# Splitting each weight tile with a casting DMA and an accumulating DMA in a one-core decoder step

## The chip, the cores and the metric

The kernel runs on one core of one Trainium2 chip. The metric is the device time of one execution in microseconds (us), the median of the runs.

## What is computed

One inference step of a decoder trunk with one layer, for a prompt of 1024 tokens and 8 sample tokens (T = 1032 in all), model width 1024, in float32:

```python
h = rms_norm(x, g_mix)
z = h @ w_in                                   # 1024 -> 6400
a_lin, a_gate, q, k, v, g_a, g_b = jnp.split(z, SPLITS, axis=-1)
u = a_lin * jax.nn.sigmoid(a_gate)
c, new_conv = causal_dwconv(hist_conv, u, w_dw, b_dw)      # 31 taps
out_a = jax.nn.silu(layer_norm(c, ln_g, ln_b)) @ w_conv_out
...                                            # attention: three dilated window groups of four heads
mix = jax.nn.sigmoid(g_a) * out_a + jax.nn.sigmoid(g_b) * out_b
x = x + mix @ w_out
up, new_ffn = causal_dwconv(hist_ffn, rms_norm(x, g_ffn) @ w_up, w_fdw, b_fdw)
gate, val = jnp.split(up, 2, axis=-1)
x = x + (jax.nn.silu(gate) * val) @ w_down
```

The sample rows also read caches of keys, values and convolution states. The outputs hold those caches shifted by one position, so the old rows are copied from DRAM to DRAM.

## The kernel before

**Products.** Every product is made in three passes, so that it keeps the accuracy of float32: a weight tile and the activations are each split into a high part, rounded to the type fp32r, and a low part, the float32 value less the high part. `product` (L193 to L206) adds, for every block of 128 input channels k, the matmuls high·high, high·low (of the activations) and low·high into one PSUM bank. The tokens stand in NC3 = 3 groups of CW = 344, and one weight tile of 128 x 1024 float32 (512 KB) gives 8 x 3 x 3 = 72 matmuls.

**Weights.** There are 134 such tiles: 50 of `w_in`, then 2, 8, 8, 44 and 22 of the other matrices. The first five (ag0, al0, ag1, al1, ag2) are loaded and split by code of their own. The other 129 go through `load_w`: `fetch_w` lets the SP queue load the tile to `raw` (two buffers), `split_w` makes `hi` on ScalarE with a Copy into fp32r and `lo` on VectorE as raw - hi. There are WB = 3 buffers each for `hi` and `lo`, so tile n can be written once the matmuls of tile n - 3 are done. Both instructions have a raised priority (EARLY).

**Caches.** `cache_jobs` is a list of copies from DRAM to DRAM (`o_k...`, `o_v...`, `o_convs`, `o_ffns`). Each third `load_w` (PACE = 3) takes one of them and puts it on the SP queue; `after(d, ...)` (L155) orders it behind the tile's own load d on that queue.

**The order of work.** The Tile framework schedules the program with a simulated timeline and fixes one order per engine. Each engine and each issuing queue (SP, and POOL, the GpSimd queue) works through its order strictly: an instruction that waits holds up everything behind it. A DMA also waits for the eighth one before it on its kind of queue. Four PSUM banks (tag "mm") hold the outputs of the input projection; VectorE empties those of the linear half `al` (L477, into `u`), ScalarE those of the gate `ag` (L474, into `sg`).

**What runs beside.** While the input projection runs on TensorE, VectorE does the 31-tap convolution (`conv_wide`, L484 to L503): 30 instructions for each of 8 channel blocks. Its first step, `history()` (L431), loads the convolution state with two DMAs on the SP queue (`hist`, L434), multiplies it by the taps (L437) and sums it (L441). The stores of `u`, the loads `cu` of the convolution and most of the other traffic between SBUF and DRAM are issued on POOL (L480, L488 and others).

The stages on TensorE follow each other as: first blocks ag0, al0, ag1, then al1, ag2 (to 68 us), then al2, ag3, al3, ... al7, the queries, keys and values q0, k0, v0, ... v5 with the attention between them, the gates ga and gb, the branch outputs, the output projection xo, and the ConvFFN with its blocks ug, uv and wd.

Of the kernel before, what the change touches and what calls it, by code (L numbers as in the profile page):

```python
# [10 lines left out]
F32 = mybir.dt.float32  # L11
# [5 lines left out]
P = 128  # L17
# [39 lines left out]
class Queue:  # L57
    """an engine; while `held` its instructions keep the order of the program"""

# [17 lines left out]
def trunk_step(ctx: ExitStack, tc: tile.TileContext, A: dict):  # L77
# [34 lines left out]
    def advance(queue):  # L112
        """one step of a stream of background work; an entry is a function (one step) or a generator"""
        while queue:
            if callable(queue[0]):
                queue.popleft()()
                return
            try:
                next(queue[0])
                return  # L120
            except StopIteration:
                queue.popleft()
# [25 lines left out]

    # ------------------------------------------------------------ weights and products
    cache_jobs = []  # L150
# [4 lines left out]
    def after(first, then):  # L155
        """orders two instructions of one queue"""
        if first is not None:
            tc.add_manual_dep(
                then.ins, first.ins.name,
                mybir.DependencyInfo(mybir.DependencyClass.NoSync, mybir.DependencyReason.DATA),  # L160
                reason="order",
            )
# [7 lines left out]
    def fetch_w(src, name):  # L170
        raw = wp.tile([P, 1024], F32, tag="raw", name=f"raw_{name}")
        return raw, nc.sync.dma_start(raw, src)
# [11 lines left out]
    def load_w(src, name, extra=False):  # L184
        raw, d = fetch_w(src, name)
        w = split_w(raw, name, extra)
        n_weights[0] += 1
        if n_weights[0] % PACE == 0 and cache_jobs:
            dst, s = cache_jobs.pop(0)
            after(d, nc.sync.dma_start(dst, s))  # L190
        return w

    def product(ps, w, off, xh, xl, c, ks=None, late=False):  # L193
        """three passes for every k; late: those with the weights' low part at the end"""
        n = len(xh)
        sl = cs(c) if isinstance(c, int) else c
        m = sl.stop - sl.start
        ks = ks or range(n)
        passes = [(k, i) for k in ks for i in range(3)]
        if late:  # L200
            passes = [(k, i) for k in ks for i in range(2)] + [(k, 2) for k in ks]
        for k, i in passes:
            wk = w[i // 2][:, (off + k) * P:(off + k + 1) * P]
            xk = (xl if i == 1 else xh)[k][:, sl]
            ins = nc.tensor.matmul(ps[:, :m], wk, xk, start=(k == 0 and i == 0), stop=(k == n - 1 and i == 2))  # L205
        return ins  # L206

    def mm_blocks(jobs, xh, xl):
        """jobs: (weights, first 128 rows in them, name, evacuation(c, psum)); group by group over all jobs."""
        for c in range(NC3):  # L210
            for w, off, name, evac in jobs:
                ps = bank(f"{name}_{c}")
                product(ps, w, off, xh, xl, c)
                evac(c, ps[:, :CW])
                pump()

    def mm_wide(jobs, xh, xl, order):
        """as mm_blocks, with one evacuation of all groups: evac(psum [128, 3, CW])."""
        tiles = [wide(name) for _, _, name, _ in jobs]
        for j, c in order:  # L220
            w, off, _, evac = jobs[j]
            product(tiles[j][:, c, :], w, off, xh, xl, c)
            if c == NC3 - 1:
                evac(tiles[j][:, :, :CW])
# [6 lines left out]

    # ------------------------------------------------------------ norms
    mean_col = const.tile([P, 1], F32, name="mean_col")
# [10 lines left out]
    def offsets(n):  # L244
        """the token tiles of n tokens; the last may overlap the one before"""
        return [*range(0, n - P + 1, P)] + [n - P] * (n % P > 0)
# [10 lines left out]
    def rsqrt(ps, tmp):  # L257
        """1 / sqrt(ps + EPS), with one Newton step after the approximate root"""
        y, r, u = tmp
        act.activation(y, ps, AF.Sqrt, bias=eps_col)  # L260
        dve.reciprocal(r, y)
        dve.scalar_tensor_tensor(u, r, -0.5, r, ALU.mult, ALU.mult)
        dve.scalar_tensor_tensor(y, ps, EPS, u, ALU.add, ALU.mult)
        dve.scalar_tensor_tensor(r, y, 1.5, r, ALU.add, ALU.mult)
        return r
# [5 lines left out]
    def spread(r, name, behind=None, n=CW, d=None):  # L271
        """[token, tile] -> the tokens' row over all partitions, in PSUM."""
        offs = offsets(n)
        m = len(offs)
        d = (scratch(f"diag_{name}", "sm", m * P) if d is None else d).rearrange("p (a b) -> p a b", a=m)
        dve.tensor_tensor(
            out=d,
            in0=ident.unsqueeze(1).broadcast_to([P, m, P]),
            in1=r.unsqueeze(2).broadcast_to([P, m, P]),
            op=ALU.mult,  # L280
        )
        ps = bank(f"sp_{name}", "s")
        for j, off in enumerate(offs):
            after(behind, nc.tensor.matmul(ps[:, off:off + P], onesm, d[:, j, :], start=True, stop=True))
        return ps[:, :n]
# [21 lines left out]

    # ------------------------------------------------------------ first norm
    x_in = A["xT"]
# [24 lines left out]

    # of the first weights the part that the first products need comes first
    raw0 = scratch("raw_ag0", "ca", T)[:, :1024]
# [13 lines left out]
    def scaled_split(c, ks=range(KB), g=G_MIX):  # L350
        """x · g in two parts; a token's factor is left to the evacuations"""
        for k in ks:
            xk = xs[k][:, cs(c)]
            act.activation(hh[k][:, cs(c)], xk, AF.Copy, scale=pv[:, g, k:k + 1])
            dve.scalar_tensor_tensor(hl[k][:, cs(c)], xk, pv[:, g, k:k + 1], hh[k][:, cs(c)].bitcast(F32),
                                     ALU.mult, ALU.subtract)
# [23 lines left out]

    # the first blocks' products do not wait for the norm's factors
    R1, R2 = (0, 1, 2), (3, 4)
# [39 lines left out]

    # ------------------------------------------------------------ constants and the caches' copies
    wdw = load_const("w_dw", [P, KB, 31])
# [34 lines left out]

    # ------------------------------------------------------------ branch A: GLU and wide convolution  # L460
    u_dram = [dram.tile([P, T], F32, name=f"u_dram{k}") for k in range(KB)]
# [6 lines left out]
    def glu(j, sg=None, u=None):  # L468
        """the gate's and the linear half's evacuation, and the stores"""
        sg = sg or slot(f"sg{j}")  # L470
# [50 lines left out]

    # ------------------------------------------------------------ branch B: attention
    def perm(ap, g):
# [37 lines left out]
    def attention_unit(g, p):  # L561
# [93 lines left out]
        def sample_scores():  # L655
            """the sample rows against the cached keys and their own"""
            kc = slot(f"kc{b}", F32, NS * (P + 1)).rearrange("p (b j) -> p b j", b=NS)
# [29 lines left out]
    def combine(p):  # L687
# [21 lines left out]
        nc.scalar.activation(st[:, 1:4], st[:, 1:4], AF.Exp)  # L709
        # samples: one softmax over the three groups' keys, which weighs the groups by their denominators  # L710
        sst = small.tile([2 * NS, 4], F32, tag="sst", name=f"sst{p}")
# [33 lines left out]
    def sample_out(p):  # L745
        """the sample rows' weighted values, with the weights spread over a head's channels"""
        while taps:
# [17 lines left out]

    # ------------------------------------------------------------ LayerNorm of the convolution's output
    c_norm = []
# [41 lines left out]

    # ------------------------------------------------------------ gates  # L810
    sa_dram = [dram.tile([P, T], F32, name=f"sa_dram{k}") for k in range(KB)]
# [127 lines left out]

    # the second norm's factor of a token is left to the evacuations  # L940
    h2h, h2l = mh, ml
# [14 lines left out]

    # ------------------------------------------------------------ ConvFFN
    def narrow_conv(o, z, name):
# [30 lines left out]
    def up_first(blocks):  # L989
        """the first blocks, group by group"""  # L990
        ws = [w_first] + [load_w(A["w_up"][o], name) for o, name in blocks[1:]]
# [39 lines left out]

    # ------------------------------------------------------------ last products and norm, group by group
    s3 = slot("s3")
# [54 lines left out]

    # the last group leaves with its tokens over the partitions, where their factor is a column
    turned, yg = [], {}  # L1090
# [161 lines left out]
```

## Time and profile before

| what | value |
|---|---|
| time, median of 2 runs | 1676.63 us (1675.12 and 1678.14) |
| span of the profiled execution, first to last instruction | 1673.9 us |
| the profiled execution's own time | not given apart from its span; the runs' median is 2.7 us above the span |
| TensorE matmul busy | 1654.8 us, 99% of the span |
| VectorE busy | 1081.3 us, 65% |
| ScalarE busy | 522.4 us, 31% |
| GpSimd busy | 113.8 us, 7% |
| moved by DMA | 197.40 MB, of which 141.99 MB on SP's queue and 53.81 MB on POOL's |

A busy share is an average over stages that have different limits. A copy from DRAM to DRAM counts once in the bytes moved. Matmul rows overlap: each shows 0.32 us, but one starts every 0.157 us.

### The profile page before, as it was taken

Reading aid. Unit: us, or ns where it says so; the run is one execution under the profiler, and the core shown is the slowest. Engines: PE = TensorE matmul, PEld = TensorE weight load, DVE = VectorE, ACT = ScalarE, POOL = GpSimd, SP = SyncE. Lnnn points to the kernel's source line nnn. Section 1 sums busy time; section 2 is a strip of 40 time slices with the busy share of each in tenths; the row PEclk is TensorE's granted clock in tenths of the full one; section 3 lists DMA queues with packets and bytes.
Section 4 is the critical chain, followed back from the end, with each engine's and each line's share of the span. In section 5 each row is a group of like instructions: output and inputs, shape, how many; then the busy total and the mean of one; then the engine's idle time right before and its main releaser. Section 6 shows DMA issues by size and latency. Waiting matters only on the chain.

```text
span 1673.9 us, 25134 instructions
## 1 busy us (share of the span) xinstructions
PE 1654.8 (99%) x10564; PEld 1615.6 (97%) x10564; DVE 1081.3 (65%) x1594; ACT 522.4 (31%) x889; POOL 113.8 (7%) x174
## 2 busy tenths in 40 slices
PE   8999999999999999999999999999999999999997
PEld 8999998898898999999999999999999999999997
DVE  5889998798996996754346554544543553553466
ACT  6411123344433324542224322212221221221243
POOL 0101011011111102110000000000000000000002
PEclk9999999999999999999999999999999999999998
DMA  8544322332335439783531221222221221222112
GB/s 296 187 127 128 119 88 80 100 104 65 103 132 174 155 134 294 222 319 124 216 114 45 80 74 68 76 82 82 76 76 64 101 76 66 74 101 75 65 54 102
DMA packets 69264, 197.40 MB, mean 118 GB/s; under 512 B 8080, under 2 KB 29616, under 8 KB 69152
## 3 DMA queue, kind: packets, MB, share of 16 engines
q1 hardware_dynamic: 53376, 141.99, 25.8%
q0 software_dynamic: 15776, 53.81, 9.6%
q8 instruction: 83, 1.36, 0.3%
q14 instruction: 29, 0.24, 0.0%
HBM read 164.29 MB, written 76.61 MB: 144 GB/s over the span
## 4 chain that ended last, share of the span: by engine, by line
PE 93%; DVE 2%; issue 2%; DMA 1%; ACT 0%; SPq 0%; POOL 0%; DVEq 0%; POOLq 0%; ACTq 0%
PE uv L205 14%; PE ug L205 14%; PE dn L205 12%; PE ga L205 6%; PE xo L205 5%; PE v L205 4%; PE k L205 4%; PE q L205 4%; PE al L205 4%; PE oa L205 4%; PE gb L205 4%; PE ag L205 3%; PE first L205 3%; PE s L603 2%; PE up L205 2%; PE dl L205 2%
## 5 line engine op out<-in xcount | busy, mean ns | idle before, releaser
L493 DVE SCALAR_TENSOR_TENSOR ca<-cu,c_w_dw,ca 128x1019 f32<-128x1019 f32 (+22 forms) x240 | 300.4, 1268 | 1.7
L205 PE MATMUL uv<-mh,hi_uv 128*128 128x344 f32 x504 | 161.2, 320 | 0.0
L205 PE MATMUL uv<-mh,lo_uv 128*128 128x344 f32 x504 | 160.9, 319 | 0.0
L205 PE MATMUL uv<-ml,hi_uv 128*128 128x344 f32 x504 | 160.5, 318 | 0.0
L205 PE MATMUL ug<-mh,hi_ug 128*128 128x344 f32 x480 | 153.4, 320 | 0.0
L205 PE MATMUL ug<-mh,lo_ug 128*128 128x344 f32 x480 | 153.2, 319 | 0.0
L205 PE MATMUL ug<-ml,hi_ug 128*128 128x344 f32 x480 | 152.8, 318 | 0.0
L205 PE MATMUL dn<-gh,lo_wd 128*128 128x344 f32 x456 | 145.8, 320 | 0.0
L205 PE MATMUL dn<-gl,hi_wd 128*128 128x344 f32 x456 | 145.6, 319 | 0.1
L205 PE MATMUL dn<-gh,hi_wd 128*128 128x344 f32 x456 | 145.6, 320 | 0.0
L923 DVE TENSOR_TENSOR xr<-dn,xr 128x1032 f32<-128x1032 f32 x42 | 51.8, 1233 | 99.0 <-PE dn L205 99.0
L205 PEld LDWEIGHTS uv<-ml,hi_uv 128*128 128x128 f32 x504 | 94.7, 188 | 0.0
L205 PEld LDWEIGHTS uv<-mh,lo_uv 128*128 128x128 f32 x504 | 94.7, 188 | 0.0
L205 PEld LDWEIGHTS uv<-mh,hi_uv 128*128 128x128 f32 x504 | 94.5, 188 | 0.0
L205 PEld LDWEIGHTS ug<-ml,hi_ug 128*128 128x128 f32 x480 | 90.2, 188 | 0.0
L205 PEld LDWEIGHTS ug<-mh,lo_ug 128*128 128x128 f32 x480 | 90.2, 188 | 0.0
L205 PEld LDWEIGHTS ug<-mh,hi_ug 128*128 128x128 f32 x480 | 90.0, 188 | 0.0
L205 PEld LDWEIGHTS dn<-gl,hi_wd 128*128 128x128 f32 x456 | 85.7, 188 | 0.4 <-DVE gl L67 0.4
L205 PEld LDWEIGHTS dn<-gh,lo_wd 128*128 128x128 f32 x456 | 85.6, 188 | 0.0
L205 PEld LDWEIGHTS dn<-gh,hi_wd 128*128 128x128 f32 x456 | 85.6, 188 | 0.0
L67 ACT ACTIVATE hi_ug<-raw_ug 128x1024 fp32r<-128x1024 f32 x22 | 23.4, 1064 | 144.3 <-PE dn L205 92.3
L67 ACT ACTIVATE hi_uv<-raw_uv 128x1024 fp32r<-128x1024 f32 x22 | 23.4, 1063 | 127.1 <-PE ug L205 83.9
(725 smaller groups left out, 4403.7 us busy)
## 6 DMA issues: line engine op xcount, KB each, us to landing
o_k<-cache_k SPq DMA_DIRECT2D x16, 1023.5 KB, 7.2
o_v<-cache_v SPq DMA_DIRECT2D x16, 1023.5 KB, 6.2
raw_ug<-w_up SPq DMA_DIRECT2D x22, 512.0 KB, 3.5
raw_uv<-w_up SPq DMA_DIRECT2D x22, 512.0 KB, 3.5
raw_wd<-w_down SPq DMA_DIRECT2D x22, 512.0 KB, 3.4
xrow<-x_rows SPq DMA_DIRECT2D x9, 512.0 KB, 6.0
x<-xT SPq DMA_DIRECT2D x24, 172.0 KB, 5.2
u_dram<-u POOLq DMA_DIRECT2D x8, 516.0 KB, 3.0
```

The lines of the kernel that those rows point to most:

```text
L67: ins = op(*args, **kwargs)
L205: ins = nc.tensor.matmul(ps[:, :m], wk, xk, start=(k == 0 and i == 0), stop=(k == n - 1 and i == 2))
L493: after(anchor[0], nc.vector.scalar_tensor_tensor(acc[:, d:SEQ], u[:, :SEQ - d], w[:, 30 - d:31 - d], acc[:, d:SEQ], ALU.mult, ALU.add))
L603: nc.tensor.matmul(sps[:, :nk], q[hs, i * P:(i + 1) * P], k[hs, k0:k0 + nk], start=True, stop=True)
L923: nc.vector.tensor_tensor(out=v3(t), in0=ps, in1=v3(t), op=ALU.add)
```

## The change

`load_w` no longer loads `raw`. A DMA on POOL loads the tile into `hi`, whose type is fp32r, so that this DMA casts. ScalarE then writes the negative of `hi` to `lo`, and a second DMA on POOL loads the same tile again and adds it to `lo`. VectorE has no part in it. The copy of the caches stays on SP, but is no longer ordered behind a weight load. The other lines of the diff take out comments; they and the longer `load_w` move the line numbers behind it by seven.

```diff
     def load_w(src, name, extra=False):
-        raw, d = fetch_w(src, name)
-        w = split_w(raw, name, extra)
+        if extra:
+            hi, lo = (ph[0].tile([P, T], F32R, tag="gl", name=f"{n}_{name}", bufs=GB)[:, :1024] for n in ("hi", "lo"))
+        else:
+            hi, lo = (wp.tile([P, 1024], F32R, tag=n, name=f"{n}_{name}", bufs=WB) for n in ("hi", "lo"))
+        d = nc.gpsimd.dma_start(hi, src)
+        with tc.high_priority(EARLY):
+            act.activation(lo, hi.bitcast(F32), AF.Copy, scale=-1.0)
+            nc.gpsimd.dma_start(lo, src, accum_op=ALU.add)
         n_weights[0] += 1
         if n_weights[0] % PACE == 0 and cache_jobs:
             dst, s = cache_jobs.pop(0)
-            after(d, nc.sync.dma_start(dst, s))
-        return w
+            nc.sync.dma_start(dst, s)
+        return hi, lo
```

Since the scheduler sets the orders, they move more than the diff tells. On the SP queue, behind the load of the last tile that `fetch_w` still loads (raw_ag2), there stood before:

```order
L172 DMA raw_ag2_293<-w_in 128x1024
L1127 DMA o_ffns<-state_ffn 128x8x44
L172 DMA raw_al2_823<-w_in 128x1024
L172 DMA raw_ag3_928<-w_in 128x1024
L172 DMA raw_al3_1023<-w_in 128x1024
L190 DMA o_k128<-cache_k128 128x8x254
L172 DMA raw_ag4_1120<-w_in 128x1024
L172 DMA raw_al4_1212<-w_in 128x1024
L434 DMA hist0_855<-conv_hist 128x960
L434 DMA hist1_888<-conv_hist 128x960
```

The same place of the SP queue now, where x4 and x16 are four and sixteen copies in a row:

```order
L172 DMA raw_ag2_293<-w_in 128x1024
L197 DMA o_k128<-cache_k128 128x8x254
L197 DMA o_v128<-cache_v128 128x8x254
L197 DMA o_k512<-cache_k512 128x2x1022 x4
L197 DMA o_v512<-cache_v512 128x2x1022 x4
L197 DMA o_k2048<-cache_k2048 128x2047 x16
L197 DMA o_v2048<-cache_v2048 128x2047 x16
L197 DMA o_convs<-state_conv 128x8x232
L1134 DMA o_ffns<-state_ffn 128x8x44
L441 DMA hist0_854<-conv_hist 128x960
L441 DMA hist1_887<-conv_hist 128x960
```

All 44 copies of the caches have moved together, ahead of the two loads of `hist`; before, two of them stood there.

On VectorE, where the outputs of al2 are multiplied into u2, the new order is:

```order
L484 TENSOR_TENSOR u2_818<-al2_0_828,sg2_153 128x344
L444 TENSOR_TENSOR hist0_854<-hist0_854,c_w_dw_790 128x240 x4
L484 TENSOR_TENSOR u2_818<-al2_1_858,sg2_153 128x344
L444 TENSOR_TENSOR hist1_887<-hist1_887,c_w_dw_790 128x240 x2
L448 TENSOR_REDUCE hsum_800<-hist0_854 128x32
L444 TENSOR_TENSOR hist1_887<-hist1_887,c_w_dw_790 128x240 x2
L504 SCALAR_TENSOR_TENSOR hr0_1335<-cu0_959,c_w_dw_790,hsum_800 128x8
L504 SCALAR_TENSOR_TENSOR hr1_1715<-cu1_1340,c_w_dw_790,hsum_800 128x8
L484 TENSOR_TENSOR u2_818<-al2_2_889,sg2_153 128x344
```

The multiplications of `hist0` stand between the evacuations of al2's first and second token group; before, they stood behind the second one's.

On POOL the new order at the same time is:

```order
L190 DMA hi_al2_823<-w_in 128x1024
L487 DMA u_dram0_801<-u0_150 128x1032
L488 DMA o_u<-u0_150 128x38
L190 DMA hi_ag3_927<-w_in 128x1024
L487 DMA u_dram1_802<-u1_152 128x1032
L488 DMA o_u<-u1_152 128x38
L190 DMA hi_al3_1021<-w_in 128x1024
L193 DMA lo_al2_824<-w_in 128x1024
L495 DMA cu0_959<-u_dram0_801 128x1032
L193 DMA lo_ag3_928<-w_in 128x1024
L495 DMA cu1_1340<-u_dram1_802 128x1032
L193 DMA lo_al3_1022<-w_in 128x1024
```

The three loads of `hi` and the three of `lo` are new on this queue; the accumulating load of al2's low part stands behind the store of u1, which waits for the products of ag2 and al1.

## Rows read from the trace of the kernel before

**Rows 1.** The page: the span, and busy time, share and instructions of each engine.

```profile
span 1673.9 us, 25134 instructions
...
PE 1654.8 (99%) x10564; PEld 1615.6 (97%) x10564; DVE 1081.3 (65%) x1594; ACT 522.4 (31%) x889; POOL 113.8 (7%) x174
```

**Rows 2.** TensorE's waits, longest first: us in total, times, longest.

```profile
PE first L205 <- ACT hh L67: 5.6, 1, 5.6
PE turned L1099 <- ACT yg L1095: 3.3, 2, 3.1
```

**Rows 3.** Timeline of TensorE: start, duration of one row.

```profile
68.06 0.32 PE L205 MATMUL al<-hh,hi_al 128*128 128x344 f32 x1
...
86.92 0.32 PE L205 MATMUL ag<-hh,lo_ag 128*128 128x344 f32 x1
```

**Rows 4.** Timeline of the SP queue: issue time, length of the issue.

```profile
43.46 0.33 SPq L172 DMA_DIRECT2D raw_ag<-w_in  x1
...
47.57 0.58 SPq L190 DMA_DIRECT2D o_k<-cache_k  x1
...
71.68 0.90 SPq L434 DMA_DIRECT2D hist<-conv_hist  x2
```

**Rows 5.** DMA issues: count, KB each, median us from issue to landing.

```profile
o_k<-cache_k SPq DMA_DIRECT2D x16, 1023.5 KB, 7.2
...
raw_ug<-w_up SPq DMA_DIRECT2D x22, 512.0 KB, 3.5
...
u_dram<-u POOLq DMA_DIRECT2D x8, 516.0 KB, 3.0
cu<-u_dram POOLq DMA_DIRECT2D x8, 516.0 KB, 5.1
...
cn<-c_dram POOLq DMA_DIRECT2D x8, 516.0 KB, 13.8
...
o_k<-cache_k SPq DMA_DIRECT2D x4, 1022.0 KB, 8.9
...
o_k<-cache_k SPq DMA_DIRECT2D x1, 1016.0 KB, 7.6
...
o_convs<-state_conv SPq DMA_DIRECT2D x1, 928.0 KB, 6.3
...
o_ffns<-state_ffn SPq DMA_DIRECT2D x1, 176.0 KB, 5.1
```

**Rows 6.** Windows: length, busy of five engines, PEclk, DMA share, GB/s (last two columns).

```profile
1027.00:1030.00 3.00, 3.00 (x21) 3.00 (x20) 1.83 (x3) 1.07 (x1) 0.00 (x0) 1.00 0.99 411
...
20.00:30.00 10.00, 10.00 (x67) 10.00 (x67) 7.93 (x20) 8.20 (x18) 0.00 (x0) 1.00 1.02 372
...
640.00:660.00 20.00, 20.00 (x130) 20.00 (x129) 13.73 (x30) 8.59 (x12) 5.81 (x11) 1.00 0.98 314
```

**Rows 7.** Timeline of VectorE around the convolution state.

```profile
75.82 0.52 DVE L477 TENSOR_TENSOR u<-al,sg 128x344 f32<-128x344 f32 x1 [0.24 <-PE al L205]
76.49 1.37 DVE L437 TENSOR_TENSOR hist<-hist,c_w_dw 128x240 f32<-128x240 f32 x4 [0.16 <-DMA hist<-conv_hist]
```

**Rows 8.** Timeline of POOL's issues after the first blocks.

```profile
68.18 0.58 POOL L480 DMA_DIRECT2D u_dram<-u  x1 [6.75 <-DVE u L420]
```

**Rows 9.** The two splitting instructions, by tile: duration ns min/median/max.

```profile
L67 ACT ACTIVATE hi_ug<-raw_ug x22: 1057/1063/1068, 865.2 to 1565.8; 128x1024 fp32r<-128x1024 f32 x22
L67 DVE TENSOR_TENSOR lo_ug<-raw_ug,hi_ug x22: 1215/1217/1226, 866.3 to 1567.1; 128x1024 fp32r<-128x1024 f32 x22
```

**Rows 10.** Timeline of ScalarE: the split of the last weight tile, wd53.

```profile
1622.70 1.06 ACT L67 ACTIVATE hi_wd<-raw_wd 128x1024 fp32r<-128x1024 f32 x1 [3.98 <-PE dn L205]
```

**Rows 11.** Windows of the attention stage: columns as in rows 6.

```profile
200.00:300.00 100.00, 100.00 (x629) 91.66 (x628) 90.35 (x127) 32.02 (x77) 11.54 (x16) 1.00 0.32 93
300.00:400.00 100.00, 100.00 (x654) 89.08 (x654) 85.02 (x160) 40.70 (x120) 13.26 (x17) 1.00 0.30 86
400.00:500.00 100.00, 100.00 (x664) 90.74 (x663) 90.44 (x165) 39.95 (x125) 13.01 (x21) 1.00 0.33 109
```

## The prediction

> **What bounds the kernel now.** I read the page's busy times first. TensorE is busy for 1654.8 of 1673.9 us [rows 1]. So at most 19 us could be won without taking matmuls away, and the change takes none. Next I read TensorE's waits: the longest are 5.6 us at the start and 3.3 us at the end [rows 2]. No weight is late anywhere in between. VectorE's 1081 us and ScalarE's 522 us are covered by TensorE, so what the change takes from them is worth nothing directly. The question is what it makes late. The timeline of TensorE gives the pace: from the first matmul of al2 at 68.06 us to the one at 86.92 us there are 120 matmuls, one per 0.157 us [rows 3]. A token group of 24 takes 3.8 us, a weight tile of 72 takes 11.3 us. With three buffers, tile n's buffer comes free two tiles before tile n is wanted: 22.6 us.
>
> **Part 1: work taken away.** 129 VectorE subtractions of 1.217 us go, 157 us in all; ScalarE keeps 129 copies of 1.063 us, now from `hi` to `lo` [rows 9]. Both lie beside TensorE. I put the gain at 0. The bound: between 200 and 500 us, where VectorE is about 90% busy, the weight-load row of TensorE idles 8.3 + 10.9 + 9.3 = 28.5 us [rows 11]. If all of that were VectorE's doing, 28.5 us come back.
>
> **Part 2: the two DMAs of a tile in steady state.** From a free buffer to a ready `lo` there are four steps: the casting load, ScalarE's copy, POOL's two issues of some 0.53 us each, and the accumulating load. The trace shows neither kind of load. The nearest row is POOL's 516 KB load `cu`, 5.1 us to landing; SP's 512 KB load takes 3.5, POOL's store 3.0, and its slowest load in traffic, `cn`, 13.8 [rows 5]. With `cu` for both: 5.1 + 1.1 + 1.1 + 5.1 = 12.4 us, against 22.6. With 13.8 for the accumulating one it is 21.1, still inside. I take 0 for the steady state. The cover is gone once that load takes over 22.6 - 7.3 = 15.3 us.
>
> Three places have less than 22.6 us. At the end of xo, three tiles are worked group by group. wo5's buffer comes free 7.6 us before xo ends, and uv0 is wanted 3.8 us after it: 11.4 us, so uv0 is about 1 us late. ug1's `hi` is queued on POOL behind uv0's `lo`, so it is issued 7.3 us after wo5 is free and ready at 7.3 + 12.4 = 19.7, wanted at 15.1: together 5 us. wd53 is the second: its buffer is freed just before ScalarE's 1622.70 us [rows 10], and four blocks of 440 tokens (12 matmuls each, 12 x 0.157 x 440/344 = 2.4 us) come before it, 9.6 us against 12.4: 3 us. Third, ScalarE waits for each casting load with its evacuations queued behind it, and in the attention stage TensorE follows ScalarE closely. Eighteen tiles q, k and v by 5.1 us would be 92 us if nothing hid it; four PSUM banks of 3.8 us each hide most, and I take 7. Together 15 us; the ends are 0 and 100.
>
> **Part 3: the copies of the caches lose their pace.** This is the large term. Before, each copy stood on SP's queue behind a weight load that waited for its buffer; the first one was issued at 47.57 us, and `hist` was issued at 71.68 us and used at 76.49 us [rows 4, 7]. Now SP has no weight loads left behind raw_ag2, and the 44 copies go out back to back, held only by the rule that eight are in flight. `hist0` stands behind all of them. On VectorE its multiplication stands ahead of al2's second evacuation, so VectorE waits, with everything behind it, until `hist0` has landed. al2 keeps two of the four PSUM banks, TensorE can still do ag3's first two groups, and then it stands at ag3's third.
>
> When does `hist0` land? The copies are 32 of 1023.5 KB, 8 of 1022, 2 of 1016, one of 928 and one of 176 (o_k's rows stand for o_v too) [rows 5]: 44,064 KB, or 45.1 MB. On SP, raw_ag2 and `hist0` add 1.0 MB. POOL's loads and stores of that time (u0, u1, cu0, cu1 and seven weight loads) add 11 x 0.52 = 5.8 MB. Sum 51.9 MB. The first copy is issued right behind raw_ag2's 43.46 us [rows 4]; with 1.1 us to the first byte, 44.9 us. (A 512 KB load lands after 3.5 us, of which 1.3 us is data at 411 GB/s; I put half the rest ahead and half behind.) The rate: a single copy moved at 411 GB/s with the DMA engines 99% busy, the start's mix of loads at 372, the busiest mixed 20 us at 314 [rows 6]. All three have full engines, so no faster rate is in sight. For some 130 us of unbroken traffic I take the middle one, 372: 139.5 us, landing at 185.5 us. The four multiplications (1.37 us) and the evacuation (0.52) [rows 7] let TensorE go on at 187.4 us. Before, it had done the same 120 matmuls at 86.9 us. Loss: 100.5 us. At 411 GB/s the loss is 87 us, at 314 it is 126.
>
> This wait hides another. lo_al2 stands on POOL behind the store of u1, issued before at 68.18 us [rows 8]. With four issues and a load among the copies it lands near 80 us, so al2 is 12 us late. But al2 and ag3's first two groups are then done by about 100 us, long before 185, so this costs nothing more.
>
> The Trainium skill (DMA: Bandwidth & Descriptors, section Latency and other measured facts) gives 207 to 214 GB/s per direction for DMA copies between HBM tensors. This case's single copy at 411 disagrees; no run here shows many in a row. By it the time would be that of rival A below.
>
> **The sum.** Span 1673.9 + 100.5 + 15 = 1789.4 us; the median lies 2.7 us above the span, so 1792 us. Its own range is 1676.6 + 87 - 28.5 + 8 = 1743 (fastest copies, all of part 1's bound, only the 8 us of the two tile places) to 1676.6 + 126 + 100 = 1903.
>
> **The rivals.**
> A, *many copies in a row run at half a single one's rate*. For it: the mixed window at 314 GB/s is already a quarter lower. Against: the single copy's rate came with the engines 99% busy, so the engines set it. At 206 GB/s the 45.1 MB take 219 us and POOL's share passes beside; `hist0` lands at 268 us, the loss is 183 us, the time 1676.6 + 183 + 15 = 1875.
> B, *the accumulating load takes over 15.3 us*. For it: nothing in the trace shows one. The Trainium skill (DMA: Bandwidth & Descriptors, Rules for kernel authors) says that an accumulating DMA reads its destination and writes it later; no run here shows that. Against: it would have to be three times `cu`. At four times, 20.4 us, a tile needs 27.7 us from free to ready, three buffers turn every (27.7 + 11.3) / 3 = 13.0 us, and 129 tiles lose 1.7 us each: 1792 + 219 = 2011.
> C, *VectorE was what paced TensorE, and its relief pays for the stall: not slower*. For it: VectorE is 90% busy from 200 to 500 us, and 157 us of it go. Against: TensorE's list has no long wait on VectorE, and the idle of its loads there is 28.5 us. It decides once more than 100.5 + 15 - 33.5 = 82 us come back, which gives 1710; with all 157 us back it is 1635.
> That the DMAs do not round as ScalarE did would change values, but neither the count nor the shapes of the matmuls, so not the time.
>
> **Chances.** The forecast 0.66, A 0.10, B 0.15, C 0.05, the rest 0.04 spread like the forecast. A change of 2%, 33.5 us, is about what a measurement of this kernel can tell from none. Forecast, A and B are all slower by more: with the rest 0.94 (a little less for unseen cover). C splits into 0.03 within 2% and 0.03 faster, rounded up. The range 1743 to 1903 holds the forecast and A and leaves out B and C, 0.2 together.
>
> **What would show it.** Right: the copies all issued between 44 and about 170 us at a full DMA share; VectorE's longest wait the one for `hist`, some 90 us; one gap on TensorE of that size in ag3, ending at 175 to 215 us, and afterwards the old pace of 11.3 us per tile. Wrong: TensorE waiting on `lo` tiles throughout (B); `hist` landing before 100 us with no gap; or TensorE in the attention stage visibly faster than before (C).

## The result, and the profile after

The changed kernel takes 1819.49 us (median of 2 runs, 1818.20 and 1820.79) against 1676.63: a ratio of 1.085 [1.082, 1.089], 143 us slower. The forecast was 1792 us, the range 1743 to 1903. The profiled execution's span is 1819.0 us, 145.1 more than the span of before.

The page's busy line, against [rows 1]:

```profile
span 1819.0 us, 25175 instructions
...
PE 1658.9 (91%) x10564; PEld 1622.2 (89%) x10564; DVE 944.6 (52%) x1465; ACT 524.7 (29%) x889; POOL 292.6 (16%) x432
```

TensorE has the same 10564 matmuls and only 4 us more of busy time, so nearly all of the 145 us is time in which it stands. VectorE lost 129 instructions (1594 to 1465), the subtractions, and 137 us; POOL rose from 114 to 293 us. TensorE's waits of after, which answer to [rows 2], and the longest of VectorE and POOL (in all, times, longest):

```profile
PE ag L212 <- DVE u L484: 105.7, 1, 105.7
PE al L212 <- DMA lo_al<-w_in: 12.6, 1, 12.6
PE ag L212 <- DMA hi_ag<-w_in: 6.3, 1, 6.3
...
PE gb L212 <- ACT sb L826: 5.6, 3, 4.2
PE gb L212 <- DMA lo_gb<-w_in: 4.6, 1, 4.6
```

```profile
DVE hist L444 <- DMA hist<-conv_hist: 117.5, 1, 117.5
```

```profile
POOL u_dram L487 <- DVE u L484: 119.7, 6, 115.5
```

One wait of 105.7 us on TensorE stands out. It names VectorE's `u`, and VectorE in turn waited 117.5 us for a DMA, the load of `hist`. POOL, with its next weight loads, stood 115.5 us behind the same `u`. The timelines of SP and VectorE say why. They answer to [rows 4, 7], where `hist` was issued at 71.68 us and used at 76.49:

```profile
32.68 0.74 SPq L197 DMA_DIRECT2D o_k<-cache_k  x1
...
59.59 72.01 SPq L197 DMA_DIRECT2D o_k<-cache_k  x16
134.56 50.85 SPq L197 DMA_DIRECT2D o_v<-cache_v  x16
188.61 0.60 SPq L197 DMA_DIRECT2D o_convs<-state_conv  x1
191.76 14.94 SPq L1134 DMA_DIRECT2D o_ffns<-state_ffn  x1
206.81 3.65 SPq L441 DMA_DIRECT2D hist<-conv_hist  x2
```

```profile
97.41 0.52 DVE L484 TENSOR_TENSOR u<-al,sg 128x344 f32<-128x344 f32 x1 [19.07 <-PE al L212]
...
215.39 1.37 DVE L444 TENSOR_TENSOR hist<-hist,c_w_dw 128x240 f32<-128x240 f32 x4 [117.47 <-DMA hist<-conv_hist]
216.68 0.51 DVE L484 TENSOR_TENSOR u<-al,sg 128x344 f32<-128x344 f32 x1
```

VectorE empties al2's first token group at 97.41 us. The next instruction in its order multiplies `hist0`, which lands at 215 us because all copies of the caches stand ahead of it on SP, the first issued at 32.68 us, the last by 206.7. al2's second group is emptied at 216.68, and TensorE goes on. The windows of that stretch (columns as in [rows 6]) show a core on which only the copies work:

```profile
120.00:140.00 20.00, 0.00 (x0) 0.00 (x0) 0.00 (x0) 0.00 (x0) 0.00 (x0) 0.50 1.02 321
...
180.00:200.00 20.00, 0.00 (x0) 0.00 (x0) 0.00 (x0) 0.00 (x0) 0.00 (x0) 0.50 1.01 312
```

The DMA engines are full (share 1.01) and move 312 to 321 GB/s. These are the large copies, 32 with rows of 8188 bytes. Ten with shorter rows went ahead of them, two of 1016 bytes and eight of 4088. While those eight ran, with POOL's loads beside them, the engines were as full and moved less:

```profile
44.90:60.00 15.10, 15.10 (x100) 15.10 (x99) 11.75 (x24) 8.29 (x14) 1.84 (x3) 1.00 1.08 213
60.00:80.00 20.00, 11.06 (x63) 9.74 (x61) 17.09 (x34) 10.17 (x18) 3.11 (x6) 0.79 1.06 222
```

The large copies land 27 to 29 us after their issue, against 7.2 in [rows 5]; the loads of the weights, in the ConvFFN, after 3.8 us (casting) and 5.2 us (accumulating):

```profile
o_k<-cache_k SPq DMA_DIRECT2D x16, 1023.5 KB, 29.0
o_v<-cache_v SPq DMA_DIRECT2D x16, 1023.5 KB, 27.0
hi_ug<-w_up POOLq DMA_DIRECT2D x22, 512.0 KB, 3.8
lo_ug<-w_up POOLq DMA_DIRECT2D x22, 512.0 KB, 5.2
```

To place the loss, read off the trace's timeline when TensorE starts the first matmul of q0, ga0 and oa0, and take differences. This table holds every kernel below; the last stretch ends with the span.

| kernel | start to q | q to ga | ga to oa | oa to end |
|---|---|---|---|---|
| before | 192.3 | 298.0 | 232.2 | 951.4 |
| after | 324.8 | 290.1 | 244.7 | 959.4 |
| e1_behind | 258.2 | 303.2 | 243.3 | 958.3 |
| e2_paced | 197.8 | 290.0 | 245.7 | 957.9 |
| e3_before_unpaced | 319.7 | 296.6 | 237.7 | 952.4 |
| e4_nocopies | 194.3 | 290.0 | 242.8 | 957.9 |
| e5_sp_loads | 195.7 | 294.7 | 243.4 | 960.6 |
| e6_dve_back | 198.2 | 294.6 | 237.8 | 957.2 |
| e7_three | 317.6 | 290.1 | 246.4 | 959.5 |
| e8_four | 199.7 | 290.6 | 245.4 | 959.5 |
| e9_one | 396.1 | 290.0 | 245.9 | 960.2 |
| e10_qkv | 194.6 | 294.2 | 229.2 | 952.8 |
| e11_gb | 192.7 | 297.9 | 236.3 | 952.0 |
| e12_qkv_gates | 194.4 | 294.6 | 240.8 | 951.2 |

Of the 145 us, 132.5 are lost before q, in the stretch of the copies. The attention stage gains 8, the gates lose 12.5, the rest loses 8. Each row is one execution. The attention stage repeats well (290.0 to 290.1 us in five kernels), the gates less so.

### The profile page after: what moved, and what is told of

It is laid out like the page before. It is cut to its first block, busy times and chain, and to the rows that moved or that the text cites. A ratio compares the mean times of both kernels' runs of the same rounds, so it can differ in the third digit from the quotient of the medians.

```text
span 1819.0 us, 25175 instructions
## 1 busy us (share of the span) xinstructions
PE 1658.9 (91%) x10564; PEld 1622.2 (89%) x10564; DVE 944.6 (52%) x1465; ACT 524.7 (29%) x889; POOL 292.6 (16%) x432
## 4 chain that ended last, share of the span: by engine, by line
PE 74%; DMA 14%; issue 7%; DVE 3%; SPq 1%; POOL 1%; ACT 0%; DVEq 0%; POOLq 0%
PE uv L212 13%; PE ug L212 12%; PE dn L212 11%; DMA o_k<-cache_k 6%; PE ga L212 4%; PE k L212 4%; PE v L212 4%; PE q L212 4%; PE oa L212 4%; PE al L212 3%; DMA o_v<-cache_v 3%; PE ag L212 3%; DMA pb<-pp_dram 2%; PE up L212 2%; PE s L610 2%
## 5 line engine op out<-in xcount | busy, mean ns | idle before, releaser
L500 DVE SCALAR_TENSOR_TENSOR ca<-cu,c_w_dw,ca 128x1001 f32<-128x1001 f32 (+23 forms) x240 | 301.2, 1268 | 3.3
L212 PE MATMUL ag<-hh,hi_ag 128*128 128x344 f32 x120 | 39.6, 330 | 112.0 <-DVE u L484 105.7
L212 PEld LDWEIGHTS ag<-hh,hi_ag 128*128 128x128 f32 x120 | 23.5, 196 | 112.7 <-DVE u L484 106.0
```

What stands on the lines that cost most here:

```text
L500: after(anchor[0], nc.vector.scalar_tensor_tensor(acc[:, d:SEQ], u[:, :SEQ - d], w[:, 30 - d:31 - d], acc[:, d:SEQ], ALU.mult, ALU.add))
```

## The experiments

**The copies alone, and the path alone.** Theory 1: the loss is the copies, unpaced and ahead of `hist` on SP. Rival 2: it is the two new DMAs of each weight tile. Four kernels separate them.

e3_before_unpaced takes the kernel before and drops one thing:

```diff
-            after(d, nc.sync.dma_start(dst, s))
+            nc.sync.dma_start(dst, s)
```

> The kernel before, with ScalarE's and VectorE's split and no casting or accumulating DMA; only the ordering of each copy behind its tile's load is dropped, so that the scheduler puts some 40 copies on SP ahead of raw_al2, raw_ag3, raw_al3 and hist. Theory 1: the copies alone make the loss. al2's tile itself is now behind them, so TensorE stands from ag2's end (68 us) until they have landed, at 316 GB/s near 190 to 215 us: a loss of 100 to 145 us, 1780 to 1820 us. Rival 2: within 10 us of 1677 us, since no weight goes through the new DMAs.

Measured: 1807.05 us, ratio 1.077 [1.075, 1.079]. The loss appears without any casting or accumulating DMA, 127.4 us of it before q. Here the copies stand ahead of the load of al2 itself:

```profile
PE al L205 <- ACT hi_al L67: 119.0, 2, 116.9
```

```profile
126.66 34.39 SPq L190 DMA_DIRECT2D o_v<-cache_v  x11
164.03 0.33 SPq L172 DMA_DIRECT2D raw_al<-w_in  x1
```

e4_nocopies takes the changed kernel and leaves the copies out:

```diff
-        if n_weights[0] % PACE == 0 and cache_jobs:
-            dst, s = cache_jobs.pop(0)
-            nc.sync.dma_start(dst, s)
```

> The changed kernel without the copies of the caches (the outputs o_k, o_v, o_convs and o_ffns lack their old rows): everything else of the change stays. Theory 1: 1675 to 1695 us, the small places only; no wait over 10 us at hist. Rival 2: 1780 us or more.

Measured: 1689.31 us, ratio 1.007 [1.005, 1.009]. So everything else of the change costs 11 to 13 us.

e2_paced keeps the copies and gives them their pace again, on POOL:

```diff
-            nc.sync.dma_start(dst, s)
+            after(d, nc.gpsimd.dma_start(dst, s))
```

> The changed kernel, with each copy of the caches issued on POOL behind its tile's own casting load, so that the pace of before is back. Theory 1: neither the wait for hist nor a burst is left; what remains of the change are the small places of some 25 us (15.5 of them in the stage of gb, which I put down to weight loads queued on POOL behind other loads that wait) less the 8 us that the attention stage gained: 1677 to 1700 us. Rival 2: 1780 us or more, since every weight tile still goes through both DMAs.

Measured: 1690.82 us, ratio 1.008 [1.006, 1.009]. All the bytes of the changed kernel are moved, every tile goes through both DMAs, and 128.7 us are back. Theory 1 holds, rival 2 falls.

e1_behind keeps the unpaced burst on SP, but orders it behind `hist` and the rope tables:

```diff
-            nc.sync.dma_start(dst, s)
+            after(sp_gate[0], nc.sync.dma_start(dst, s))
...
-            nc.sync.dma_start(rope_s, A["rope"][1])
+            sp_gate[0] = nc.sync.dma_start(rope_s, A["rope"][1])
```

> The changed kernel, with the copies of the caches left on SP in one burst, but ordered behind the loads of hist and of the rope tables on that queue. Theory 1 (the loss of 143 us is the copies standing ahead of hist on SP): hist lands near 75 us as before and the wait of 117.5 us on VectorE is gone. The burst of 45 MB is still there, at about 316 GB/s some 143 us long, and POOL's weight loads landed in 11 to 20 us during it in the changed kernel; a tile then takes 30 to 40 us from a free buffer to a ready low part against the 22.6 us that three buffers give, so 0 to 4 us are lost on each of about 13 tiles, 0 to 50 us. Time 1685 to 1735 us. Rival 2 (the casting and accumulating DMAs themselves cost most of it): 1780 us or more.

Measured: 1764.99 us, ratio 1.052 [1.051, 1.054], 30 us above the upper end that theory 1 gave. The wait for `hist` is gone, yet 65.9 of the 132.5 us before q stay. Now TensorE waits for weights, in small pieces:

```profile
PE ag L213 <- DMA lo_ag<-w_in: 22.7, 4, 11.7
PE al L213 <- DMA hi_al<-w_in: 9.7, 1, 9.7
PE al L213 <- DMA lo_al<-w_in: 7.4, 2, 4.1
PE ag L213 <- DVE u L485: 6.7, 1, 6.7
```

In this kernel's stretch from 68 to 250 us the weight loads land after 10.9 to 15.8 us (medians):

```profile
hi_al<-w_in POOLq DMA_DIRECT2D x5, 512.0 KB, 15.8
lo_ag<-w_in POOLq DMA_DIRECT2D x5, 512.0 KB, 12.0
lo_al<-w_in POOLq DMA_DIRECT2D x5, 512.0 KB, 10.9
hi_ag<-w_in POOLq DMA_DIRECT2D x4, 512.0 KB, 14.0
```

With these a tile needs 14 to 16 for the casting load, some 2.5 for ScalarE and POOL's two issues and 11 to 12 for the accumulating load, 27 to 30 us, against the 22.6 of the prediction's part 2, so tile after tile is late. The burst does harm in two ways, and taking away only its place in the queue gives back half of what is lost before q. What matters is the pace.

**At what rate do the copies move?** The prediction's largest choice was 372 GB/s; the row of large copies above shows about 316. e7_three issues all 44 copies in one loop, orders `hist` behind the last and lets each copy wait for the third before it; e9_one is the same with the one before it. The core of e7's edit:

```diff
+        c = nc.sync.dma_start(dst, s)
+        if len(flying) >= 3:
+            tc.add_manual_dep(
+                c.ins, flying[-3].ins.name,
+                mybir.DependencyInfo(mybir.DependencyClass.Sync, mybir.DependencyReason.DATA),
+                reason="three",
+            )
+        flying.append(c)
```

> The changed kernel with all 44 copies still on SP ahead of hist, but each made to wait for the third before it, so that three are in flight in place of eight. In the changed kernel the copies alone moved at 307 to 328 GB/s with the DMA engines full, a single one at 422 to 434. Theory 7 (many copies in flight slow each other): the copies alone move at 370 GB/s or more, hist is used by 175 to 195 us in place of 215, and the time is 1780 to 1800 us. Rival 8 (any unbroken row of such copies moves at some 316): 300 to 330 GB/s, hist at 210 to 225 us, 1810 to 1830 us. Should three not fill the engines, their share falls below 0.95 and the rate says nothing.

Measured: 1813.59 us, ratio 1.080 [1.078, 1.082]. While TensorE stands, the windows show

```profile
160.00:180.00 20.00, 0.00 (x0) 0.00 (x0) 0.00 (x0) 0.00 (x0) 0.00 (x0) 0.50 1.01 316
180.00:200.00 20.00, 0.00 (x0) 0.00 (x0) 0.00 (x0) 0.00 (x0) 0.00 (x0) 0.50 1.01 305
```

Full engines, the same rate: three in flight are no faster than eight. Rival 8's rate and time hold; `hist` was used at 230 us, 5 us past its bound. The time alone would not decide: VectorE's order differs here, and its wait for `hist` starts at 139 us rather than 98.

> The kernel with the 44 copies on SP ahead of hist once more, each made to wait for the one before it, so that one is in flight. Eight in flight moved at 307 to 328 GB/s with full DMA engines, three at 305 to 316. Theory 11 (a copy from DRAM to DRAM moves at some 316 GB/s whatever is beside it, and the window of before that showed 411 held part of a weight load): the 1 us windows in which a copy alone fills the engines show 290 to 335 GB/s. Rival 12 (a lone copy is faster, and even two or three in flight slow each other): 400 GB/s or more in those windows. By either the gaps between copies make the run longer: with 6 to 7 us a copy, hist is used at 310 to 360 us, the time 1890 to 1950 us.

Measured: 1894.05 us (one run), inside the range; `hist` was used at 303 us, 7 us before the expected stretch, after a wait of 188.5 us on VectorE. One copy in windows of 1 us:

```profile
224.00:225.00 1.00, 0.00 (x0) 0.00 (x0) 0.00 (x0) 0.00 (x0) 0.00 (x0) 0.50 0.91 131
225.00:226.00 1.00, 0.00 (x0) 0.00 (x0) 0.00 (x0) 0.00 (x0) 0.00 (x0) 0.50 0.62 262
226.00:227.00 1.00, 0.00 (x0) 0.00 (x0) 0.00 (x0) 0.00 (x0) 0.00 (x0) 0.50 1.02 434
227.00:228.00 1.00, 0.00 (x0) 0.00 (x0) 0.00 (x0) 0.00 (x0) 0.00 (x0) 0.50 0.53 221
```

The peak of 434 is rival 12's number. The whole copy costs 0.91 + 0.62 + 1.02 + 0.53 = 3.08 us of all engines for 1.048 MB, 340 GB/s. (A window counts a packet's whole time where the packet starts.) The trace's single packets show what lies behind this. A copy is 128 packets of 8188 bytes. Here the first sixteen take 0.91 us on the mean and the others 0.309, which is 424 GB/s for 16 engines.

The 411 of [rows 6] is not the fast part of such a copy. In the kernel before, that copy's packets all start between 1027.07 and 1029.94 us, right behind those of a weight tile, which still has 184 KB in the first of these windows:

```profile
1027.00:1028.00 1.00, 1.00 (x8) 1.00 (x7) 0.96 (x2) 0.00 (x0) 0.00 (x0) 1.00 1.04 422
1028.00:1029.00 1.00, 1.00 (x9) 1.00 (x8) 0.66 (x1) 0.30 (x1) 0.00 (x0) 1.00 1.04 434
1029.00:1030.00 1.00, 1.00 (x8) 1.00 (x7) 0.20 (x1) 0.76 (x1) 0.00 (x0) 1.00 0.90 377
```

Its packets take 0.315 us on the mean, the first sixteen 0.331: no slow start, 416 GB/s for the whole copy. In the row of the changed kernel (120 to 200 us) such packets take 0.418 us on the mean, and five in six take more than 0.315; with three in flight (e7, 150 to 200 us) the mean is 0.418 too. So it is rival 12's account that the packets bear out: with several copies in flight most packets take longer, and the start of a copy is not what makes the row slow. Why they take longer stays open.

**The 11 to 13 us that remain.** In e4 and e2 the start loses 2.0 and 5.5 us, the gates 10.6 and 13.5, the end 6.5 in both, and attention gives 8. In e2 the gates' loss sits at gb:

```profile
PE gb L212 <- ACT sb L826: 9.8, 2, 8.4
```

```profile
659.71 0.29 DVE L765 CUSTOM_DVE_ANT_0 pb<-pb,vc 128x129 f32<-128x129 f32 x1 [11.81 <-DMA vc<-vT]
...
662.73 1.06 ACT L303 ACTIVATE sq_lv<-cn 128x1032 f32<-128x1032 f32 x1 [14.12 <-issue]
```

```profile
640.00:660.00 20.00, 16.10 (x102) 15.54 (x100) 5.95 (x25) 4.21 (x7) 5.62 (x10) 1.00 1.05 331
660.00:680.00 20.00, 13.18 (x65) 12.74 (x65) 17.30 (x47) 11.45 (x14) 6.10 (x10) 0.66 0.96 268
```

TensorE's stop ends at 665.42 us, behind an evacuation `sb` on ScalarE. Ahead of that `sb` ScalarE had stood 14.1 us before a square of the LayerNorm (`sq_lv`). The profile names no releaser (`issue`), but VectorE writes its input `cn` right before, from 661.42 us on, and VectorE itself had waited 11.8 us for the load `vc`, in a stretch with full DMA engines. In the kernel before VectorE has such a wait too (9.3 us) and TensorE doesn't stop; why it does here isn't shown. ScalarE's waits for casting loads (18.4 us in this stage, the longest, 9.7, ending at 630.71 us) cost TensorE no stop there. After the stop TensorE's granted clock averages 0.66 over 20 us. In the changed kernel itself the stops at gb are a mixture: 4.6 us for `lo_gb`, 4.2 us behind the same squares, and 0.8 us right behind a wait of 6.0 us for a casting load. The profiled e2 is the longest of its four runs (1693.28 us), so its stages add up to 17.5 us where the medians give 12.8. Three ideas were tried on e2, and three mixtures on the kernel before.

e5_sp_loads takes loads that wait off POOL:

```diff
-                nc.gpsimd.dma_start(pb[h * HALF:(h + 1) * HALF], pp_dram[p][h, g].partition_broadcast(HALF))
+                nc.sync.dma_start(pb[h * HALF:(h + 1) * HALF], pp_dram[p][h, g].partition_broadcast(HALF))
...
-            nc.gpsimd.dma_start(d, c_dram[k])
+            nc.sync.dma_start(d, c_dram[k])
```

> The paced kernel (copies on POOL behind the tile's casting load), with the loads pb and cn of the gb stage moved from POOL to SP, whose queue holds little there. The gb stage takes 98.0 us before and 111.6 us in the paced kernel. Theory 3 (weight loads stand on POOL behind loads that wait for VectorE and for full DMA engines): the stage falls to 98 to 101 us, the time to 1677 to 1681 us. Rival 4 (the stage loses because the DMA engines are full there, whichever queue issues): it stays at 108 to 113 us, the time at 1687 to 1693 us.

Measured: 1695.16 us, ratio 1.010 [1.009, 1.012]. From gb's first matmul to ob's the stage takes 105.2 us, between the two expectations, but ob behind it takes 4.1 us longer than in e2, attention 4.7, and the whole is no faster. So theory 3 carries at most half of gb's own loss (6.4 of 13.6 us) and nothing of the whole.

e6_dve_back puts the subtraction back on VectorE:

```diff
-            act.activation(lo, hi.bitcast(F32), AF.Copy, scale=-1.0)
-            nc.gpsimd.dma_start(lo, src, accum_op=ALU.add)
+            dve.tensor_tensor(out=lo, in0=raw, in1=hi.bitcast(F32), op=ALU.subtract)
```

> The paced kernel with one half of the change undone: hi still comes by the casting DMA, but lo is raw less hi on VectorE again (raw by its own load on SP); no copy of hi on ScalarE, no accumulating DMA. From the first q to the first ga TensorE needed 298.0 us before and 290.0 us in the paced kernel. Theory 5 (VectorE's relief gave those 8 us): the stretch is back at 296 to 299 us. Rival 6 (they came from the weights' path, loads earlier or ScalarE): it stays at 289 to 291 us. Whole time 1678 to 1695 us by the first, 1670 to 1685 us by the second.

Measured: 1689.06 us, ratio 1.007 [1.006, 1.008]; q to ga takes 294.6 us, between both. Some 4.6 of the 8 us go with this edit, which gives VectorE its work back and also takes away ScalarE's copies and the accumulating loads; the other 3.4 don't depend on it.

e8_four gives the tiles up to the branch outputs a fourth pair of buffers:

```diff
+        elif n_weights[0] % 4 == 3 and n_weights[0] < 47:
+            hi, lo = fourth("hx", name), fourth("lx", name)
```

> The paced kernel with a fourth pair of weight buffers for the tiles up to the branch outputs (every fourth tile there uses it; room comes from one of the two raw buffers and two small tiles). From the first gb matmul to the first oa matmul TensorE needed 122.1 us before, 137.2 us in the paced kernel. Theory 9 (the change lost the two raw buffers, into which SP loaded two tiles ahead; a load now waits for a free hi, and a slow one is late): with one more tile ahead the stretch falls to 122 to 128 us, the time to 1672 to 1683 us. Rival 10 (depth doesn't matter, full DMA engines or the new order of VectorE's and ScalarE's work cost it): 134 to 139 us, 1686 to 1694 us.

Measured: 1699.43 us, ratio 1.014 [1.012, 1.016]; gb to oa takes 136.0 us (599.7 to 735.7). Theory 9 falls: with this fourth pair gb is hardly faster than in e2 (137.2). Why the whole is slower than e2 and than rival 10's range stays open; the edit also takes a raw buffer and shrinks two small tiles.

In e10, e11 and e12 the kernel before keeps its own path and its paced copies, and only some tiles go through the DMAs (their copies then follow on POOL):

```diff
+        by_dma = name[0] in "qkv"
```

> The kernel before, with the casting and accumulating DMAs for the 18 tiles of q, k and v alone; the other 111 load_w tiles keep raw, ScalarE and VectorE, and every copy of the caches keeps its place behind a load. From the first q to the first ga TensorE needs 298.0 us before and 290.0 us with the whole change paced; from the first ga to the first oa 232.2 and 245.7 us. Theory 13 (each stage's gain or loss belongs to that stage's own weight path): 289 to 292 and 231 to 235 us, the time 1668 to 1674 us, a little faster than before. Rival 14 (TensorE runs ahead in the attention stage to work of other engines that is no earlier, and the gates give it back): 289 to 292 and 238 to 243 us, the time 1676 to 1682 us.

Measured: 1672.73 us, ratio 0.997 [0.995, 0.998]: a third of a per cent below before, and the fastest kernel here. Attention gives 3.8 us rather than 6 to 9, and the gates give 3.0 more. Rival 14, that the gates give back what attention gains, falls here; of theory 13 the time holds, while both stages lie outside its ranges. In this stage VectorE is busy for 245.7 us, against 264.0 before and 265.6 in e6, so it is relieved; yet the stage takes the same 294 us as e6 (and 294.7 in e5, where VectorE is relieved too). VectorE's subtractions of q, k and v are therefore not what the last 4 us hang on; what it is stays open.

> The kernel before, with the casting and accumulating DMAs for the 8 tiles of gb alone. From the first gb to the first oa TensorE needs 122.1 us before and 137.2 us with the whole change paced. Theory 13: the loss is gb's own weight path, 132 to 138 us, the time 1686 to 1694 us. Rival 14: 121 to 126 us, 1676 to 1682 us.

Measured: 1681.66 us, ratio 1.002 [1.001, 1.003]; gb to oa takes 126.1 us, 4 more than before, where theory 13 wanted 132 to 138 and rival 14 up to 126: here theory 13 falls and rival 14's numbers hold within 0.1 us. gb's own path is a quarter of the 15.1 us that e2 loses there.

> The kernel before with the casting and accumulating DMAs for q, k, v, ga and gb, 34 tiles in all. From the first q to the first oa TensorE needed 530.2 us before, 523.4 with the DMAs for q, k and v alone, 534.2 (126.1 of it from gb to oa) with them for gb alone, and 535.7 with the whole change paced. Theory 15 (the small loss behind the attention is made by these 34 tiles together): 533 to 538 us, the time 1680 to 1688 us. Rival 16 (it needs the change in the tiles before q or behind gb too): 522 to 529 us, the time 1671 to 1678 us.

Measured: 1683.14 us, ratio 1.003 [1.002, 1.004]; q to oa takes 535.4 us. Theory 15's numbers hold: q, k, v, ga and gb together give the net loss of that stretch (e2: 535.7). Its parts differ, though: attention gains 3.4 us here and 8.0 in e2, the gates lose 8.6 here and 13.5 there. So the net doesn't need the tiles before and behind, but it isn't shown that they have no part in the parts. TensorE's longest wait is again at gb:

```profile
PE gb L214 <- ACT sb L828: 9.6, 2, 8.2
```

Which of the 34 tiles does it is not settled beyond this: with q, k and v alone there is a gain of 6.8 us, with gb alone a loss of 4.0, with all of them a loss of 5.2.

## Why the prediction was right, point by point

- **What bounds the kernel.** TensorE; the change takes no matmul and its busy time stayed. Right.
- **Part 3, the mechanism.** Copies back to back, `hist` behind them, VectorE waiting with al2's second evacuation behind it, TensorE standing inside ag3: each step is in the traces above, and e3 and e2 show it by making the loss without the new DMAs and undoing it with them. Before `hist` lands TensorE also waits 6.3 us for a `hi_ag` and 12.6 us for lo_al2, which it can use at 92.06 us, where the prediction had it land near 80; al2's first group is emptied 25 us later than before (97.41 against 72.04 us), not 12. As forecast this costs nothing more.
- **Part 3, the size.** The mis-sized term is the copies' rate, "I take the middle one, 372". `hist0` was used at 215.39 us, where its landing was forecast for 185.5; by the same reckoning 51.9 MB over 215.4 - 1.1 - 44.9 = 169.4 us are 306 GB/s. TensorE went on at 217.24 us, a loss of 130 us against 100.5. The other 2 us before q are the low clock at the restart, which the prediction left out: 15 matmuls there take 4.5 us instead of 2.4.
- **The choice behind it.** The row that I kept as the lower end (314, loss 126 us) came nearest, in part by luck. The first copy was issued at 32.68 us and not behind 43.46, which the reckoning doesn't have; against this, while the copies with shorter rows ran, the windows from 44.9 to 80 us show 213 and 222 GB/s. Only the 32 large ones ran at 312 to 321. The 411 was right for the copy that it was read from, and wrong for a row: with several in flight each packet takes 0.418 us on the mean rather than 0.315. The prediction's "no faster rate is in sight" held; that a slower one was in store didn't show in one copy alone.
- **The signs.** The copies went out from 32.7 to 206.7 us (44 to 170 was given), VectorE waited 117.5 us for `hist` (some 90), and TensorE's gap ended at 217 us, 2 us past the 215 given. The attention stage is 8 us faster, a sign that the prediction had put down to rival C.
- **Part 1, gain 0.** Wrong in size by 8 us, well inside its bound of 28.5: attention takes 290 us rather than 298 (in e2, e4, e7 and e9 too). Whether VectorE's relief did it, rival C's mechanism, isn't shown: e6 gives 4.6 us of it back with the subtractions, but e10 and e12 have VectorE relieved in this stage and take as long as e6. At a tenth of the 82 us that rival C needed, C falls either way.
- **Part 2, steady state 0.** Right. 3.8 + 1.1 + 1.4 + 5.2 = 11.5 us per tile against 22.6, where 12.4 was the estimate, and the ConvFFN keeps its old pace.
- **Part 2, three tight places, 15 us.** From oa on 8.0 us are lost, the same as the 8 put there, but not in the same places: 2.5 from oa to xo, 3.7 from xo to uv (5 forecast for uv0 and ug1) and 1.8 behind (3 forecast for wd53). The third, ScalarE waiting for casting loads with evacuations behind, was put in the attention stage with 7 us. TensorE shows no wait of that kind there. What came instead is a loss of 12.5 us from ga to oa. Its largest stops are a late `lo_gb` (4.6 us, where part 2 had put lateness in steady state at 0) and one of 4.2 us behind ScalarE's squares, which the prediction doesn't have. So the sum of 15 us is near the 8 + 12.5 - 8 = 12.5 measured by luck, not term by term.
- **Rival A**, 206 GB/s for all, falls by the time and by 305 to 321 in the rows of large copies with three or eight in flight; the stretch of those with shorter rows, 213 and 222, is near it. The Trainium skill (DMA: Bandwidth & Descriptors, Latency and other measured facts) gives copies between HBM tensors 207 GB/s per direction at a row pitch of 512 KiB, and 214 at 4 MiB with 4 KiB of padding. The large copies here, with another layout, move more than that. **Rival B** falls: the accumulating load takes 5.2 us in the ConvFFN; only beside the burst of copies does it pass the 15.3 us of this rival (13.0, 19.7 and 20.9 us in the changed kernel), and there TensorE stands for `hist` anyway.

With the measured sizes in the places of the forecast ones the sum is 1676.6 + 132.5 - 8 + 12.5 + 8 = 1821.6 us, against 1819.5 for the median and 1820.8 for the run that they were read from.

## What to carry to other kernels

A transfer that is tied behind another load has a pace. Untie it and it goes out at once; whatever stands behind it on its queue then waits for all of it, and whatever is loaded meanwhile lands two to four times later (here 10.9 to 15.8 us against 3.8 and 5.2). Look at the new order of the issuing queue first, and then at the full DMA share. For a long row of transfers, take the rate from a row of the same kind with several in flight, or from the lowest row with full engines. A full DMA share on a single transfer doesn't say that a row will keep its rate.

## What was not expected of the hardware

- A copy of 1.048 MB that starts on idle engines has sixteen slow first packets (0.91 us against 0.309) and comes to 340 GB/s over its engine time; right behind a weight load it came to 416. With three or eight in flight a packet takes 0.42 us on the mean, 313 GB/s, and three are not faster than eight.
- One copy at a time, with the gap between them, still averages two thirds of the 316 GB/s, 203 and 207 in two windows of 40 us. One of them in e9:

```profile
200.00:240.00 40.00, 0.00 (x0) 0.00 (x0) 0.00 (x0) 0.00 (x0) 0.00 (x0) 0.50 0.58 203
```

- After a stop TensorE's clock is the lower of its two levels (0.50) and its first matmuls follow each other at 0.29 us rather than 0.157, for some 3.5 us here and 4.5 us after the long stop. From the timeline of after, behind the wait for lo_al2:

```profile
92.51 0.49 PE L212 MATMUL al<-hh,hi_al 128*128 128x344 f32 x1
92.80 0.49 PE L212 MATMUL al<-hl,hi_al 128*128 128x344 f32 x1
...
95.63 0.33 PE L212 MATMUL al<-hh,lo_al 128*128 128x344 f32 x1
95.80 0.32 PE L212 MATMUL al<-hh,hi_al 128*128 128x344 f32 x1
```
